# A hybrid decoder layer on one core: equal tile offsets modulo 1024 bytes, first loads on one queue, the first norm's residual a block ahead

## The chip, the core and the metric

The kernel runs on one core of one Trainium2 chip. The metric is device time in microseconds (us) of one execution, the median of several runs. The engines spoken of are TensorE (PE, with its weight loads shown apart as PEld), VectorE (DVE), ScalarE (ACT), GpSimd (POOL) and SyncE (SP), which issues most DMAs in order from one queue.

## The reference, cut to what matters

One layer over 512 tokens of width 1024 in fp32. A combined projection feeds three token mixers: forgetting attention ("FoX", 8 heads), a Mamba-2 scan ("SSD") and a complex diagonal state space model ("S5"). Each mixer's output is projected, gated and summed, and goes through an output projection. A norm with residual, a gated MLP (5632 up columns, width-3 convolution, 2816 down rows) and a second norm follow:

```python
proj = x @ w_in
q, k, v, f_logit, z, xbc, dt_raw, u, gate_logit = jnp.split(proj, _split_points(), axis=-1)
merged = jnp.sum(gates * jnp.einsum('blrw,rwd->blrd', branches, w_branch), axis=2)
x1  = layer_norm(ALPHA * x  + merged @ w_out, ln1_g, ln1_b)
ffn = (silu(gate) * val) @ w_down          # val, gate = split(causal_dwconv(x1 @ w_up))
out = layer_norm(ALPHA * x1 + ffn, ln2_g, ln2_b)
```

## The kernel before, in words

**Arithmetic.** Each fp32 operand of a big product is split into a high part (fp32r) and the rest, and a product takes three matmuls, hi·hi, hi·lo and lo·hi. `mm3` (lines 173 to 175) is that triple with the weight tile as the stationary operand (128 x 128) and a 512-column activation tile moving. `gemm_N` (lines 279 to 281) is the triple the other way round: a 128-column slice of x is stationary and a weight tile moves; so are the output projection (lines 1193 to 1195) and the down projection (lines 1250 to 1252).

**Where operands lie.** Four pools share each partition of SBUF, one after the other: the "ring" (`ringp`: 5 tiles `whi` and 5 tiles `wlo` of 4096 bytes, into which the stream of weights is split), `tiny` (small tiles, each taking 32 bytes or a multiple; one of them is `mn`), `xpool` (4 tiles of 8192 bytes: the split input `xth`/`xtl`, later `x1Th`/`x1Tl`, at the end the weights `resh`/`resl`) and `half` (61 "slots" of 2048 bytes: everything else of 512 columns, the split activations `ya`, `yb`, `yc`, `gy`, `mT`, `hT` and the split output weights `wkh`/`wkl` among them). In the built programs:

| pool, tile | start, before | modulo 1024 | start, after | modulo 1024 |
|---|---|---|---|---|
| ring, first `whi` / `wlo` | 28,544 / 49,024 | 896 | 28,544 / 49,024 | 896 |
| xpool, first tile | 71,424 | 768 | 71,552 | 896 |
| slots, first | 104,192 | 768 | 104,320 | 896 |

All tiles of a pool have the same remainder, since their sizes are multiples of 1024. Within a tile a stationary slice starts at a multiple of 512 bytes and a moving row at a multiple of 2048.

**Stages.** `Stream` (lines 51 to 108) loads weight tiles in a fixed order on the SP queue into two raw buffers (`wraw`), splits each on ACT (high part, line 100) and DVE (rest, line 101), and runs a few tiles ahead. `fill_first` multiplies the first four weight tiles (`w_u`) by x as the eight tiles of x arrive: a step of it is one 128-row tile of x, with 14 matmuls. The projections follow, with the mixers' tasks put between them by a list of due units (lines 1344 on); then the merges, the output projection (`out_block`, four blocks of 128 tokens, 48 matmuls each), beside which `norm1` of the block before runs, and the MLP. A scheduler orders the instructions of each engine by priority; `tc.high_priority()` moves what stands in it ahead.

**At the start** x tile 0 is loaded on the ACT queue (line 233), the first weight tile in three pieces on SP (line 83), and between the second and third piece `W.between` (`second_x`) adds x tile 1 and the small weight `fdw`. **At the first norm** `norm1(b)` issues the two loads of its residual `xr` itself (line 1156), waits some steps, adds, takes the statistics, scales (`xh`), and later has PE transpose `xh` (line 1170) and stores it (`drx`, line 1181).

Of the kernel before, what the change touches and what calls it, by code (L numbers as in the profile page):

```python
# [16 lines left out]
P = 128  # L17
# [44 lines left out]
class Stream:  # L62
# [8 lines left out]
    def prefetch(self, n):  # L71
        nc = self.nc
        while self.made < min(n, len(self.plan)):
            key, src = self.plan[self.made]
            w = self.raw.tile([P, 1024], F32, name="wraw", tag="wraw")
            if self.made:
                nc.sync.dma_start(out=w, in_=src)
            else:

                hi = self.ring.tile([P, 1024], F32R, name="whi", tag="whi")  # L80
                lo = self.ring.tile([P, 1024], F32R, name="wlo", tag="wlo")
                for h_ in (slice(0, 256), slice(256, 512), slice(512, 1024)):
                    nc.sync.dma_start(out=w[:, h_], in_=src[:, h_])
                    nc.scalar.activation(hi[:, h_], w[:, h_], AF.Copy)  # L84
                    nc.vector.tensor_tensor(out=lo[:, h_], in0=w[:, h_], in1=hi[:, h_].bitcast(F32), op=ALU.subtract)
                    if h_.stop == 512:
                        self.between()
                r = (hi, lo)
            if key in self.keep:
                r = []  # L90
                for hf in range(2):
                    hi, lo = (self.slots.tile([P, 512], F32R, name="wk" + c_, tag="s2") for c_ in "hl")
                    ws = w[:, hf * 512:(hf + 1) * 512]
                    nc.scalar.activation(hi, ws, AF.Copy)
                    nc.vector.tensor_tensor(out=lo, in0=ws, in1=hi.bitcast(F32), op=ALU.subtract)
                    r.append((hi, lo))
            elif self.made:
                hi = self.ring.tile([P, 1024], F32R, name="whi", tag="whi")
                lo = self.ring.tile([P, 1024], F32R, name="wlo", tag="wlo")
                nc.scalar.activation(hi, w, AF.Copy)  # L100
                nc.vector.tensor_tensor(out=lo, in0=w, in1=hi.bitcast(F32), op=ALU.subtract)  # L101
                r = (hi, lo)
            self.out.append(r)
            self.made += 1
# [9 lines left out]
def hybrid_trunk_kernel(ctx: ExitStack, tc: tile.TileContext, a, out):  # L114
# [18 lines left out]
    def s2(shape, dt=F32, name="s2"):  # L133
        return half.tile(list(shape), dt, name=name, tag="s2")
# [15 lines left out]
    def tt(o, x, y, op, eng=None):  # L150
        (eng or dve).tensor_tensor(out=o, in0=x, in1=y, op=op)  # L151
# [69 lines left out]
    def load_x(k):  # L221
        xraw[k] = s2([P, L], name="xraw")
        sp.dma_start(out=xraw[k], in_=a["xT"][k])
# [4 lines left out]
    wps = ps([P, P])  # L228
    for i in range(7):
        pe.matmul(wps, wz, wz, start=True, stop=True)  # L230
    with tc.high_priority():
        xraw[0] = s2([P, L], name="xraw")
        act.dma_start(out=xraw[0], in_=a["xT"][0])
        dve.tensor_copy(xp[0][0], xraw[0])  # L234
        tt(xp[0][1], xraw[0], xp[0][0].bitcast(F32), ALU.subtract)

    def second_x():
        with tc.high_priority():
            load_x(1)
            sp.dma_start(out=fdw, in_=a["w_fd"])  # L240
            split(fd[:, :, 0:16], fd[:, :, 16:32], fdw)
        split(xp[1][0], xp[1][1], xraw[1])

    W.between = second_x
    W.prefetch(1)
    load_x(2)
    split(xp[2][0], xp[2][1], xraw[2])
# [405 lines left out]
    def s5_run(qt):  # L653
        while qt not in s5m:
            yield 1
        u_load(qt)
        yield 4
        mm_, it, om, er, ei, rho = s5m.pop(qt)
        uu = s5u.pop(qt)
        v = ps([P, 8, 64])  # L660
        for g in range(8):
            pe.matmul(v[:, g, :], it[g], uu[:, g, :], start=True, stop=True)
        yield 1
        vs = s2([P, 8, 64], name="s5V")
        act.copy(vs[LOH], v[HIH])
        act.copy(vs[HIH], v[LOH])
        yield 2
        w = s2([P, 8, 64], name="s5W")
        tt(w, v, er, ALU.mult)
        tt(vs, vs, ei, ALU.mult)  # L670
        tt(w, w, vs, ALU.add)
        sc = s2([P, 512], name="s5S")
        dve.tensor_tensor_scan(out=sc, data0=rho.rearrange("p a c -> p (a c)"), data1=w.rearrange("p a c -> p (a c)"),
                               initial=0.0, op0=ALU.mult, op1=ALU.add)
        yield 3
        sw = s2([P, 512], name="s5Sw")
        act.copy(sw[LOH], sc[HIH])
        act.copy(sw[HIH], sc[LOH])
        xx = s2([P, 8, 64], name="s5X")
        dve.memset(xx[:, :, 0:1], 0.0)  # L680
        sv, swv = (m.rearrange("p (a c) -> p a c", c=64) for m in (sc, sw))
        x1_, c63 = xx[:, :, 1:64], slice(0, 63)
        tt(x1_, sv[:, :, c63], er[:, :, c63], ALU.mult)
        tt(swv[:, :, c63], swv[:, :, c63], ei[:, :, c63], ALU.mult)
        tt(x1_, x1_, swv[:, :, c63], ALU.subtract)
        yield 6
        y = ps([P, 8, 64])
        for g in range(8):
            pe.matmul(y[:, g, :], mm_[g], uu[:, g, :], start=True, stop=False)
            pe.matmul(y[:, g, :], om[g], xx[:, g, :], start=False, stop=True)  # L690
        ysb = s2([P, 8, 64], name="s5Y")
        act.copy(ysb, y)
        yield 4
        dry = tc.dram_tile([P, 512], F32, name="dry%d" % qt)
        dst = dry.rearrange("(g h) (t c) -> t h g c", h=16, c=64)
        for t in range(8):
            sp.dma_start(out=dst[7 - t], in_=ysb[16 * t:16 * t + 16])
        yield 3
        yt = s2([P, 512], name="s5yt")
        sp.dma_start(out=yt, in_=dry)  # L700
        yield 3

        g1, g2 = s2([P, 512]), s2([P, 512], name="s5g2")
        tt(g1, yt, yt, ALU.mult, pool)
        ts(g1, g1, 0.044715, ALU.mult, 1.0, ALU.add, eng=pool)
        tt(g1, g1, yt, ALU.mult, pool)
        yield 6
        act.activation(g1, g1, AF.Tanh, scale=GELU_C)
        gy = pair("gy")
        stt(g2, g1, 1.0, yt, ALU.add, ALU.mult)  # L710
        split(gy[0], gy[1], g2)
        s5y[qt] = (g2, gy)
        yield 1
# [241 lines left out]
    def fox_min(u):  # L955
        n = (fox_units[u][1] + 1) * P
        sc = fx.pop(("rel", u))
        mn = tmp([P, 1], "mn", 7)
        dve.tensor_tensor_reduce(out=sc, in0=fx.pop(("ps", u)), in1=sc, scale=1.0, scalar=3e38,
                                 op0=ALU.add, op1=ALU.min, accum_out=mn)  # L960
        fx["sc", u] = sc, mn
# [166 lines left out]
    def output_and_ffn():  # L1128
# [12 lines left out]
        def bn(bs, hf, r):  # L1141
            dve.bn_stats(out=bs[:, hf, :], in_=r)

        def norm_scalars(bs):
# [4 lines left out]
            tt(rs, rs, mhalf[:, 0:1], ALU.pow, pool)  # L1149
            return mv[:, 0:1], rs  # L1150

        def norm1(b, o):
            xr = [s2([P, 512], name="xr") for _ in range(2)]
            bs = tmp([P, 2, 6], "bs", 4)
            for hf in range(2):
                sp.dma_start(out=xr[hf], in_=a["x"][b * P:(b + 1) * P, HS[hf]])
            yield 3
            for hf in range(2):
                stt(xr[hf], xr[hf], ALPHA, o[hf], ALU.mult, ALU.add)
                bn(bs, hf, xr[hf])  # L1160
            mean, rs = norm_scalars(bs)
            xh = [s2([P, 512], name="xh") for _ in range(2)]
            for hf in range(2):
                ts(xh[hf], xr[hf], mean, ALU.subtract, rs, ALU.mult)
            yield 9
            t = slice(b * P, (b + 1) * P)
            for hf in range(2):
                tp = ps([P, 4, P])
                for kk in range(4):
                    pe.transpose(tp[:, kk, :], xh[hf][:, kk * P:(kk + 1) * P], ident)  # L1170
                f = s2([P, 4, P], name="x1f")
                for kk in range(4):
                    k = 4 * hf + kk
                    if kk % 2:
                        act.activation(f[:, kk, :], tp[:, kk, :], AF.Identity, scale=col("ln1_g", k),
                                       bias=col("ln1_b", k))
                    else:
                        ts(f[:, kk, :], tp[:, kk, :], col("ln1_g", k), ALU.mult, col("ln1_b", k), ALU.add)
                split(x1g[hf][0][:, :, t], x1g[hf][1][:, :, t], f)
            for hf in range(2):  # L1180
                sp.dma_start(out=drx[b][:, HS[hf]], in_=xh[hf])
            yield 1
# [16 lines left out]
        def advance(g):  # L1199

            if g is not None:
                if g[1] <= 1:
                    g[1] = next(g[0], 99)
                else:
                    g[1] -= 1

        wo, prev = [], None
        for b in range(NB):
            gen = out_block(b, wo)
# [281 lines left out]
```

## Time and profile before

| | us |
|---|---|
| median of 3 runs | 882.29 |
| lowest and highest | 881.64, 882.63 |
| the profiled execution, its own time | 881.78 |
| its span, first to last instruction | 880.0 |
| PE busy in the span | 866.8 |
| DVE, ACT, POOL busy | 590.9, 378.9, 63.1 |

The page gives each engine's busy time, the groups of like instructions, and a chain of waits traced back from the last instruction. Matmuls are pipelined: a row's duration reaches past the start of the next, so the cost of one in a stream is read from the distance between starts in the timeline, not from its duration. A row of the timeline has its start and duration in us, then engine, line, operation and tiles, and in brackets what ended an idle time before it.

### The profile page before, as it was taken

The page shows a single profiled execution, that of the slowest core. Times are in us where ns is not written, and L with a number is a line of the kernel's source. Part 1 is how long each engine was busy: PE and PEld are TensorE (multiplying, and loading weights), DVE is VectorE, ACT ScalarE, POOL GpSimd, SP SyncE. Part 2 cuts the span into 40 slices and gives each one's busy share as a digit, 9 for nine tenths or more (in the row PEclk, how much of TensorE's full clock was granted, in tenths as well). Part 3 has the DMA queues.
Part 4 walks back from the last instruction along what each step waited for, and adds up shares of the span by engine and source line. Part 5 has one row for each costly group of instructions (what it writes and reads, how often), then busy time and mean ns, then how long its engine had stood idle before and what let it go on. Part 6 is the DMA issues. An engine that isn't in the chain of part 4 may idle for free.

```text
span 880.0 us, 11393 instructions
## 1 busy us (share of the span) xinstructions
PE 866.8 (98%) x4211; PEld 716.5 (81%) x4211; DVE 590.9 (67%) x1022; ACT 378.9 (43%) x629; POOL 63.1 (7%) x144
## 2 busy tenths in 40 slices
PE   9999999999999999999999999999999999999996
PEld 7788788888888888788887898888888888888885
DVE  5898987885779866777667667557755555556217
ACT  5625235453656876763225244433333333343100
POOL 0370000000202220100000000000000000000001
PEclk9999999999999999999999999999999999999999
DMA  7615443424512543262516323253422222226102
GB/s 260 226 46 172 127 145 98 134 67 139 192 55 81 189 144 112 69 214 72 191 55 235 142 83 110 95 165 122 144 96 96 96 95 86 93 90 213 48 1 96
DMA packets 58648, 107.63 MB, mean 122 GB/s; under 512 B 21824, under 2 KB 27712, under 8 KB 58592
## 3 DMA queue, kind: packets, MB, share of 16 engines
q1 hardware_dynamic: 55568, 101.66, 34.6%
q10 hardware_dynamic: 3024, 5.24, 1.6%
q8 instruction: 33, 0.54, 0.3%
q14 instruction: 23, 0.19, 0.1%
HBM read 95.35 MB, written 11.53 MB: 121 GB/s over the span
## 4 chain that ended last, share of the span: by engine, by line
PE 92%; DVE 4%; issue 1%; DMA 1%; ACT 1%; POOL 0%; DVEq 0%; POOLq 0%
PE acc L173 20%; PE acc L174 20%; PE acc L175 20%; PE ps L1252 3%; PE ps L1250 3%; PE ps L1251 3%; PE acc L1250 2%; PE acc L1251 2%; PE acc L1252 2%; PE acc L279 2%; PE acc L281 2%; PE acc L280 2%; PE acc L1193 1%; PE acc L1194 1%; PE acc L1195 1%
## 5 line engine op out<-in xcount | busy, mean ns | idle before, releaser
L101 DVE TENSOR_TENSOR wlo<-wraw,whi 128x1024 fp32r<-128x1024 f32 x125 | 154.3, 1235 | 113.8 <-ACT whi L100 113.6
L100 ACT ACTIVATE whi<-wraw 128x1024 fp32r<-128x1024 f32 x125 | 132.1, 1058 | 183.8 <-PE acc L174 130.0
L173 PE MATMUL acc<-x1Th,whi 128*128 128x512 f32 (+1 forms) x384 | 144.4, 376 | 0.0
L174 PE MATMUL acc<-x1Tl,whi 128*128 128x512 f32 (+1 forms) x384 | 144.3, 376 | 0.0
L175 PE MATMUL acc<-x1Th,wlo 128*128 128x512 f32 (+1 forms) x384 | 144.2, 376 | 0.0
L173 PE MATMUL acc<-xth,whi 128*128 128x512 f32 x336 | 134.8, 401 | 0.6 <-DVE xth L234 0.6
L174 PE MATMUL acc<-xtl,whi 128*128 128x512 f32 x336 | 133.6, 398 | 0.0
L175 PE MATMUL acc<-xth,wlo 128*128 128x512 f32 x336 | 133.5, 397 | 0.0
L175 PEld LDWEIGHTS acc<-x1Th,wlo 128*128 128x128 f32 x384 | 72.3, 188 | 14.2
L174 PEld LDWEIGHTS acc<-x1Tl,whi 128*128 128x128 f32 x384 | 72.4, 188 | 14.1
L173 PEld LDWEIGHTS acc<-x1Th,whi 128*128 128x128 f32 x384 | 72.3, 188 | 14.0
L173 PEld LDWEIGHTS acc<-xth,whi 128*128 128x128 f32 x336 | 63.7, 190 | 15.7 <-ACT whi L84 0.9
L174 PEld LDWEIGHTS acc<-xtl,whi 128*128 128x128 f32 x336 | 63.7, 190 | 14.2 <-issue 0.4
L175 PEld LDWEIGHTS acc<-xth,wlo 128*128 128x128 f32 x336 | 63.5, 189 | 14.3
L160 DVE SCALAR_TENSOR_TENSOR cv<-acc,cols,cv 128x511 f32<-128x511 f32 (+1 forms) x88 | 65.4, 746 | 2.8 <-ACT cv L1229 1.5
L151 POOL TENSOR_TENSOR lrs<-lrs,mhalf 128x1 f32<-128x1 f32 x8 | 5.9, 731 | 476.7 <-DVE lrs L155 476.7
L1252 PE MATMUL ps<-whi,hTl 128*128 128x512 f32 (+1 forms) x102 | 38.7, 379 | 0.0
L1250 PE MATMUL ps<-whi,hTh 128*128 128x512 f32 (+1 forms) x102 | 38.6, 379 | 0.0
L1251 PE MATMUL ps<-wlo,hTh 128*128 128x512 f32 (+1 forms) x102 | 38.6, 379 | 0.0
L1229 ACT ACTIVATE cv<-acc,cols 128x512 f32<-128x512 f32 x44 | 33.5, 763 | 1.9 <-PE acc L175 1.9
L1237 ACT ACTIVATE cv<-cv 128x512 f32<-128x512 f32 x22 | 13.9, 632 | 41.6 <-DVE cv L160 41.6
L160 DVE SCALAR_TENSOR_TENSOR gate<-gate,acc 128x512 f32<-128x512 f32 x24 | 16.5, 686 | 16.8 <-PE acc L175 16.8
(318 smaller groups left out, 1553.2 us busy)
## 6 DMA issues: line engine op xcount, KB each, us to landing
wraw<-w_up SPq DMA_DIRECT2D x44, 512.0 KB, 3.2
wraw<-w_gate SPq DMA_DIRECT2D x24, 512.0 KB, 3.2
wraw<-w_dn SPq DMA_DIRECT2D x22, 512.0 KB, 3.2
wraw<-w_branch SPq DMA_DIRECT2D x12, 512.0 KB, 3.2
drt<-gate ACTq DMA_DIRECT2D x18, 256.0 KB, 2.3
gate<-drt SPq DMA_DIRECT2D x18, 256.0 KB, 5.1
wraw<-w_out SPq DMA_DIRECT2D x8, 512.0 KB, 3.2
wraw<-w_xbc SPq DMA_DIRECT2D x6, 512.0 KB, 4.2
```

The source lines that it names most:

```text
L100: nc.scalar.activation(hi, w, AF.Copy)
L101: nc.vector.tensor_tensor(out=lo, in0=w, in1=hi.bitcast(F32), op=ALU.subtract)
L160: dve.scalar_tensor_tensor(out=o, in0=x, scalar=s, in1=y, op0=op0, op1=op1)
L173: pe.matmul(o, w[0], x[0], start=first, stop=False)
L174: pe.matmul(o, w[0], x[1], start=False, stop=False)
L175: pe.matmul(o, w[1], x[0], start=False, stop=last)
L279: pe.matmul(o[b], xh, wh[:, s], start=(k == 0), stop=False)
L280: pe.matmul(o[b], xh, wl[:, s], start=False, stop=False)
L1229: act.activation(r, o, AF.Identity, scale=col("ffn_w", w0 + 2), bias=col("ffn_b", ch))
L1250: pe.matmul(o, hh, wh, start=(k == 0), stop=False)
L1251: pe.matmul(o, hh, wl, start=False, stop=False)
L1252: pe.matmul(o, hl, wh, start=False, stop=(k == NF - 1))
```

## The change

It has five parts. (1) `mn` gets 11 buffers in place of 7. The four more take 4 x 32 = 128 bytes of `tiny`, so that xpool and slots start 128 bytes further on; the ring stays (table above). (2) x tile 0 is loaded on SP after the first weight piece, x tile 1 after the third piece and the next whole weight tile. (3) In `norm1` the residual of block b+1 is loaded when block b's norm begins (block 0's before the output projection). (4) That norm's arithmetic up to `xh` is put under high priority, without the pause of three steps before it. (5) In `s5_run` a pause before the GELU is 4 units, not 3.

```diff
@@ Stream.prefetch
-                for h_ in (slice(0, 256), slice(256, 512), slice(512, 1024)):
+                for n_, h_ in enumerate((slice(0, 256), slice(256, 512), slice(512, 1024))):
...
-                    if h_.stop == 512:
-                        self.between()
+                    if n_ < 2:
+                        self.between(n_)
@@ hybrid_trunk_kernel
-    with tc.high_priority():
-        xraw[0] = s2([P, L], name="xraw")
-        act.dma_start(out=xraw[0], in_=a["xT"][0])
-        dve.tensor_copy(xp[0][0], xraw[0])
-        tt(xp[0][1], xraw[0], xp[0][0].bitcast(F32), ALU.subtract)
-
-    def second_x():
+    def early(n_):
         with tc.high_priority():
-            load_x(1)
-            sp.dma_start(out=fdw, in_=a["w_fd"])
-            split(fd[:, :, 0:16], fd[:, :, 16:32], fdw)
-        split(xp[1][0], xp[1][1], xraw[1])
-
-    W.between = second_x
+            if n_ == 0:
+                load_x(0)
+                dve.tensor_copy(xp[0][0], xraw[0])
+                tt(xp[0][1], xraw[0], xp[0][0].bitcast(F32), ALU.subtract)
+            else:
+                sp.dma_start(out=fdw, in_=a["w_fd"])
+                split(fd[:, :, 0:16], fd[:, :, 16:32], fdw)
+                load_x(1)
+        if n_:
+            split(xp[1][0], xp[1][1], xraw[1])
+
+    W.between = early
@@ s5_run
         sp.dma_start(out=yt, in_=dry)
-        yield 3
+        yield 4
@@ fox_min
-        mn = tmp([P, 1], "mn", 7)
+        mn = tmp([P, 1], "mn", 11)
@@ output_and_ffn
+        xrs = {}
+        def xr_load(b):
+            xrs[b] = [s2([P, 512], name="xr") for _ in range(2)]
+            for hf in range(2):
+                sp.dma_start(out=xrs[b][hf], in_=a["x"][b * P:(b + 1) * P, HS[hf]])
+
         def norm1(b, o):
-            xr = [s2([P, 512], name="xr") for _ in range(2)]
+            xr = xrs.pop(b)
+            if b + 1 < NB:
+                xr_load(b + 1)
             bs = tmp([P, 2, 6], "bs", 4)
-            for hf in range(2):
-                sp.dma_start(out=xr[hf], in_=a["x"][b * P:(b + 1) * P, HS[hf]])
-            yield 3
-            for hf in range(2):
-                stt(xr[hf], xr[hf], ALPHA, o[hf], ALU.mult, ALU.add)
-                bn(bs, hf, xr[hf])
-            mean, rs = norm_scalars(bs)
-            xh = [s2([P, 512], name="xh") for _ in range(2)]
-            for hf in range(2):
-                ts(xh[hf], xr[hf], mean, ALU.subtract, rs, ALU.mult)
+            with tc.high_priority():
+                for hf in range(2):
+                    stt(xr[hf], xr[hf], ALPHA, o[hf], ALU.mult, ALU.add)
+                    bn(bs, hf, xr[hf])
+                mean, rs = norm_scalars(bs)
+                xh = [s2([P, 512], name="xh") for _ in range(2)]
+                for hf in range(2):
+                    ts(xh[hf], xr[hf], mean, ALU.subtract, rs, ALU.mult)
             yield 9
...
+        xr_load(0)
         wo, prev = [], None
```

The built programs show what moves at the two places of which the prediction speaks. The first is the start. On SP, the queue of loads, the kernel before has this order (xraw_108 is x tile 1, wraw_122 the second weight tile, xraw_118 x tile 2):

```order
L83 DMA wraw_99<-w_u 128x256
L223 DMA xraw_108<-xT 128x512
L240 DMA fdw_83<-w_fd 128x128
L83 DMA wraw_99<-w_u 128x256
L83 DMA wraw_99<-w_u 128x512
L77 DMA wraw_122<-w_u 128x1024
L223 DMA xraw_118<-xT 128x512
```

After the change SP has at the start (xraw_101 is x tile 0, xraw_111 x tile 1):

```order
L83 DMA wraw_95<-w_u 128x256
L223 DMA xraw_101<-xT 128x512
L238 DMA fdw_83<-w_fd 128x128
L83 DMA wraw_95<-w_u 128x256
L83 DMA wraw_95<-w_u 128x512
L77 DMA wraw_122<-w_u 128x1024
L223 DMA xraw_111<-xT 128x512
```

x tile 0 has taken the place of x tile 1, and x tile 1 now stands behind the second weight tile. On PE, at the second step of `fill_first` (x tile 1; acc_146 to acc_149 are the four products), the changed program has this order, where before each product's triple stood together behind both lines 307 and 308:

```order
L307 MATMUL ps_145<-xth_79,fd_84 32x512
L173 MATMUL acc_146<-xth_79,whi_96 128x512
L173 MATMUL acc_147<-xth_79,whi_96 128x512
L173 MATMUL acc_148<-xth_79,whi_96 128x512
L173 MATMUL acc_149<-xth_79,whi_96 128x512
L308 MATMUL ps_145<-xtl_80,fd_84 16x512
L174 MATMUL acc_146<-xtl_80,whi_96 128x512
```

The five matmuls that need only the high part of x tile 1 come first, then those that need its rest. The second place is the output projection with the first norm. On SP the difference is (- before, + after; `xr` are residual loads, `drx` the stores of the normed blocks):

```order
-L77 DMA wraw<-w_out 128x1024 x8
+L77 DMA wraw<-w_out 128x1024 x5
+L1157 DMA xr<-x 128x512 x2
+L77 DMA wraw<-w_out 128x1024 x3
 L77 DMA wraw<-w_up 128x1024
-L1156 DMA xr<-x 128x512
+L1157 DMA xr<-x 128x512
 L77 DMA wraw<-w_up 128x1024
-L1156 DMA xr<-x 128x512
-L77 DMA wraw<-w_up 128x1024 x3
-L1181 DMA drx_4656<-xh 128x512 x2
-L1156 DMA xr<-x 128x512 x2
```

Block 0's residual now stands among the output weights, and block 1's, which stood behind block 0's store, stands among the first MLP weights. On DVE the norm of block 0 reads after the change (xr_4660 and xr_4661 are its residual halves, wlo_4749 a weight tile of the MLP):

```order
L160 SCALAR_TENSOR_TENSOR xr_4660<-xr_4660,acc_4664 128x512
L160 SCALAR_TENSOR_TENSOR xr_4661<-xr_4661,acc_4665 128x512
L1142 BN_STATS bs_4786<-xr_4660 128x6
L1142 BN_STATS bs_4786<-xr_4661 128x6
L101 TENSOR_TENSOR wlo_4749<-wraw_4746,whi_4748 128x1024
L1146 BN_AGGR mv_4791<-bs_4786 128x2
L155 TENSOR_SCALAR lrs_4793<-mv_4791 128x1
L157 TENSOR_SCALAR xh_4796<-xr_4660,mv_4791,lrs_4793 128x512
L157 TENSOR_SCALAR xh_4797<-xr_4661,mv_4791,lrs_4793 128x512
```

One weight split stands inside the norm, where before there were two and a third ahead of it. On PE block 0's last matmul is the 72nd of the output projection (before: the 68th) and its transposes follow the 96th (before: the 106th); block 1's follow the 144th (before: the 145th).

## Rows read from the trace of the kernel before

**Rows 1.** The page, busy us (share of the span) and instructions.
```profile
PE 866.8 (98%) x4211; PEld 716.5 (81%) x4211; DVE 590.9 (67%) x1022; ACT 378.9 (43%) x629; POOL 63.1 (7%) x144
```
**Rows 2.** Groups on PE by shape: count | busy us, mean ns | idle before.
```profile
L173 PE MATMUL acc<-xth,whi 128*128 128x512 f32 x336 | 134.8, 401 | 0.6 <-DVE xth L234 0.6
L173 PE MATMUL acc<-x1Th,whi 128*128 128x512 f32 x320 | 126.3, 395 | 0.0
L1250 PE MATMUL ps<-whi,hTh 128*128 128x512 f32 x88 | 34.7, 395 | 0.0
L279 PE MATMUL acc<-whi,xth 128*128 128x512 f32 x64 | 25.5, 401 | 0.7 <-DVE cv L160 0.7
L1250 PE MATMUL acc<-whi,hTh 128*128 128x512 f32 x42 | 16.6, 395 | 0.0
L173 PE MATMUL acc<-yah,whi 128*128 128x512 f32 x32 | 12.7, 398 | 0.1
L173 PE MATMUL acc<-gyh,whi 128*128 128x512 f32 x16 | 6.4, 399 | 0.0
```
**Rows 3.** Timeline of PE in the MLP, ring against xpool: start us, duration.
```profile
604.16 0.39 PE L173 MATMUL acc<-x1Th,whi 128*128 128x512 f32 x1
...
617.87 0.39 PE L175 MATMUL acc<-x1Th,wlo 128*128 128x512 f32 x1
```
**Rows 4.** Timeline of PE in the last down projection, xpool against slots.
```profile
851.81 0.39 PE L1250 MATMUL acc<-resh,hTh 128*128 128x512 f32 x1
...
865.41 0.39 PE L1250 MATMUL acc<-resh,hTh 128*128 128x512 f32 x1
```
**Rows 5.** Busy us (count) in two stretches: PE, PEld, DVE, ACT, POOL, clock, DMA.
```profile
491.00:501.00 10.00, 10.00 (x46) 8.28 (x45) 6.27 (x13) 2.87 (x6) 0.54 (x1) 1.00 0.40 138
600.00:700.00 100.00, 100.00 (x432) 81.09 (x431) 58.63 (x72) 36.30 (x47) 0.00 (x0) 1.00 0.33 111
```
**Rows 6.** Timeline of PE in the output projection, slots against slots, after transposes.
```profile
478.64 1.08 PE L1170 MATMUL ps<-ident,xh 128*128 128x128 f32 x8
...
479.80 0.40 PE L1195 MATMUL acc<-wkh,mTl 128*128 128x512 f32 x1
...
481.66 0.39 PE L1194 MATMUL acc<-wkl,mTh 128*128 128x512 f32 x1
...
483.93 0.39 PE L1195 MATMUL acc<-wkh,mTl 128*128 128x512 f32 x1
```
**Rows 7.** Timeline of the start, all engines (ACTq, SPq: DMA issues).
```profile
0.71 0.41 ACTq L233 DMA_DIRECT2D xraw<-xT  x1
...
1.15 0.43 SPq L223 DMA_DIRECT2D xraw<-xT  x1
...
4.46 0.43 DVE L234 CAST xth<-xraw 128x512 fp32r<-128x512 f32 x1 [3.47 <-DMA xraw<-xT]
...
5.04 0.76 PE L173 MATMUL acc<-xth,whi 128*128 128x512 f32 x1 [0.64 <-DVE xth L234]
...
6.02 0.61 ACT L165 ACTIVATE xth<-xraw 128x512 fp32r<-128x512 f32 x1
...
8.91 1.06 ACT L100 ACTIVATE whi<-wraw 128x1024 fp32r<-128x1024 f32 x1 [0.64 <-DMA wraw<-w_u]
...
10.00 1.23 DVE L101 TENSOR_TENSOR wlo<-wraw,whi 128x1024 fp32r<-128x1024 f32 x1 [1.00 <-ACT whi L100]
...
10.38 0.39 PE L307 MATMUL ps<-xth,fd 128*32 128x512 f32 x1
```
**Rows 8.** Timeline of the norm of block 1: SP, DVE, PE.
```profile
479.43 1.20 SPq L1156 DMA_DIRECT2D xr<-x  x2
...
484.76 0.69 DVE L160 SCALAR_TENSOR_TENSOR xr<-xr,acc 128x512 f32<-128x512 f32 x1 [1.04 <-DMA xr<-x]
...
489.07 1.00 DVE L157 TENSOR_SCALAR xh<-xr,mv,lrs 128x512 f32<-128x512 f32 x2 [0.67 <-POOL lrs L151]
...
489.77 1.09 PE L1170 MATMUL ps<-ident,xh 128*128 128x128 f32 x8 [1.14 <-DVE xh L157]
```

## The prediction

> **What bounds the kernel now.** I read the page first: PE is busy for 866.8 of 880.0 us [rows 1], so nearly all the time is the sum of the distances between matmuls, and 13 us at most are waits. I then listed PE's groups by shape, to see how many matmuls there are of each kind, walked PE's timeline for the distance from start to start, and looked at the few places where PE stood still. Durations would mislead here: a 128x512 matmul is shown with about 395 ns [rows 2], but the next starts long before its end.
>
> **Part 1, the offsets.** In the MLP the moving operand lies in xpool (remainder 768) and the stationary one in the ring (896). From the first to the last row there are 59 steps [rows 3]: (617.87 - 604.16) / 59 = 232.4 ns each. In the last down projection the moving operand lies in xpool and the stationary one in a slot (both 768); from the first to the last row there are 60 steps [rows 4]: (865.41 - 851.81) / 60 = 226.7 ns. That is 5.7 ns less for the same shape and type. It is not the work of the other engines: in 491 to 501 us, where both operands are slots, DVE is busy for 63% and ACT for 29%, and PE still starts 46 matmuls in or across 10 us; in 600 to 700 us, with ring operands, DVE is busy for 59%, ACT for 36%, and PE starts only 432 in 100 us [rows 5]. Nor does it hang on an exact match: in rows 4 the stationary slices start at 0, 512, 1024 and 1536 bytes of their tile, block after block, at one distance all along. After the change every ring, xpool and slot operand stands as in rows 4 (remainder 896 throughout).
>
> How many matmuls this touches: each line of rows 2 is one of a triple, so (336 + 320 + 88 + 64 + 42) x 3 = 2550, the merges are three kinds like the ya line, 3 x 32 x 3 = 288, and the GLU adds 16 x 3 = 48. That makes 2886 of 128x512; at 5.7 ns, 16.5 us at most.
>
> Not all of them will get it. After a break (transposes, a small matmul) the short distance comes back only after some steps: the 8 steps from 479.80 to 481.66 take 1.86 us, 232.5 ns each, and the 10 steps to 483.93 take 2.27 us, 227 ns each [rows 6]. Walking PE's timeline I count 88 breaks in the streams that the change touches, most of them between 10 and 412 us, where the mixers' small matmuls stand among the projections. 88 x 8 x 5.7 ns = 4.0 us are lost so. The term is **-12.5 us**, with -16.5 (no break costs anything) and 0 as its ends. A loss I leave out, since the matmuls that already run at equal offsets are the quicker ones. PE is the bound and nothing else fills the time: DVE's 590.9 us [rows 1] leave it a third of the span, so it can follow a PE that is 1.5% quicker.
>
> The Trainium skill speaks against this term. "TensorE: Matmul & The Clock Gate", section "Step-by-step: what each phase is for", says that PE reads its moving operand and its weights through two independent ports, and that loading the next weights takes no read bandwidth from the running matmul; its section "Back-to-back issue gap" gives a gap of N/2.4 + 2.5 ns, 216 ns for 512 columns, whatever the addresses. By it this term would be 0. The trace does not agree on either count: it shows two distances, 232.4 and 226.7 ns, and neither is 216. What the page leaves possible is that the two differ for another reason than the offset, and that is the first rival below.
>
> **Part 2, the start.** PE's first real matmul starts at 5.04 us, after the split of x tile 0 that began at 4.46, when the tile had landed; its load was issued on ACT at 0.71, beside the SP queue's, where x tile 1 was issued at 1.15 [rows 7]. After the change tile 0 has SP's second place and no load competes with it but the first weight piece ahead of it. It may land up to 0.8 us sooner (the competing 256 KB of tile 1 are gone) or, if a second place lands as tile 1 did, be split as late as 6.02 [rows 7], 1.5 us later. What decides is the second step, though. It began at 10.38 and its 14 matmuls take 14 x 0.232 = 3.25 us, to 13.63. After the change tile 1 comes behind the second weight tile in SP, ACT and DVE. That weight tile was split from 8.91 on; 256 KB fewer are ahead of it now, some 0.65 us, so from about 8.25. ACT then takes 1.06 + 0.61 us (weight, tile 1), to 9.92, and DVE 1.23 us from about 9.35 for the weight and 0.69 for tile 1's rest, to 11.27 [rows 7, 8] (the 0.69 is taken from an operation of the same shape in the norm). PE runs the five high-part matmuls in between, to 11.1, and the other nine to 11.27 + 9 x 0.232 = 13.36. That is **-0.3 us**. Bounds: -1.0 if everything lands early; above, the first step took 5.34 us for 14 matmuls (5.04 to 10.38), 2.1 more than later ones, and if the wait for tile 1 makes the second step as slow, the term is +1.8.
>
> On the move to one queue the skill's "DMA: Bandwidth & Descriptors", section "Issuing engines are not separate DMA queues", says that a second issuing engine saves only the time of the issue. By it tile 0 would come later by 1.15 - 0.71 = 0.44 us, and the first matmul with it. No row of before shows the two orders side by side; the second step's sum holds either way, as it rests on tile 1.
>
> **Parts 3 and 4, the norm.** At 489.77 PE had waited 1.14 us for block 1's `xh` [rows 8]. The cause is upstream: the residual was issued at 479.43, behind block 0's store, and DVE could not add before 484.76 [rows 8]. Block 1's matmuls had ended long before: PE ran 49 more (49 x 0.227 = 11.1 us) and block 0's transposes (1.08 [rows 6]) between them and 488.63, so they ended at about 476.4. With the residual there the chain of add, statistics and scale (484.76 to 489.07 + 1.00, less a foreign 0.69: 4.6 us) can end by 481 or 482, 5 us before PE wants it. So this wait goes, -1.1. What is late next is block 0's: its last matmul is now the 72nd and its transposes follow the 96th, so 24 x 0.227 = 5.4 us cover a chain of 4.6 plus the weight split of 1.23 inside it, 5.8: +0.4. The loads on SP cost nothing as long as block 0's residual is issued while SP waits for raw buffers anyway (the sixth output weight waits for DVE's splits). Block 3's chain has 54 half-width matmuls (some 0.12 each, half of 0.23) and block 2's transposes as cover, 6.5 + 1.1 us. The term is **-0.7 us**, between -1.4 (block 0 costs nothing and a second, shorter wait goes too) and +0.5 (block 1's chain is late again by half of it).
>
> **Part 5.** The GELU's inputs are needed by the GLU much later, and POOL has 63 us of work in 880 [rows 1]: 0, with about 1 us either way for the order of the mixers' instructions on DVE and ACT that this shifts, since PE waits on those chains at times.
>
> **Sum.** -12.5 - 0.3 - 0.7 = -13.5 us. The profiled execution took 881.78 in all (its span is 880.0, and 1.8 lie around it), so 868.3; it stands 0.5 below the median of before (882.29), so **868.8 us** on the scale of the medians, 1.5% faster.
>
> **Rivals.** (a) *It is the ring, not the offset.* Every slow pair has one operand in the ring, and no fast pair has; the ring is also lower in memory and written whole tile by whole tile. If that is the reason, part 1 gives nothing, and parts 2 to 4 leave 882.3 - 1.0 = 881.3 us. For it: rows 3 and 4 can't separate the two. Against it: ring tiles and slots are parts of one memory, read by the same instructions, and the engines that write them were as busy in the quick stretch of rows 5 as in the slow one. 13%. This is also the skill's case above. (b) *Half of it.* The short distance may hold only where both slices match modulo 1024; a stationary slice of the ring moves on by 512 bytes with every triple, unlike rows 4, where it stays for 24 matmuls. The lock would then be lost and found at each step, for about half the gain: 868.8 + 6.3 = 875.1. 7%. (c) *The start is lost.* x tile 1 stands behind 512 KB that PE doesn't need yet. If it comes so late that the second step starts late and runs as slowly as the first, that costs 1.8; if tile 0 is also split at 6.02, 1.5 more. With part 1 at nothing and the norm's -0.9, the time is 882.3 + 3.3 - 0.7 = 884.9 us, slower; it decides only where (a) holds too, from a start that loses 0.7 + 1.8 = 2.5 us. For it: the order on SP. Against it: the weight tile ahead was split at 8.91, before PE wanted tile 1. 4%.
>
> **How the numbers follow.** My forecast has 76%; its own range is 864.5 to 871.5 (part 1 between -16.5 and -10, the start, the norm and the mixers' order by their bounds). The range with (b) reaches 876, and 18% or so is left outside. Within 0.2% (1.8 us) is what a measurement of this kernel can't tell from no change: (a) falls there for the most part, so faster 86%, same 9%, slower 5%.
>
> **What would show it right or wrong.** In the MLP the distance from start to start should be 227 ns over a long stretch, also in `gemm_N` and the merges; 232 there is (a), a mix is (b). The first matmul should start by 4.5 us and the second step end by 13.4; a gap of over 1 us before line 308 is (c). The transposes of block 1 should follow their matmul without a wait, and block 0's wait by under 1 us. Above 876 us part 1 is wrong; below 864 the breaks cost nothing, or PE gained where I saw no wait.

## The result and the profile after

The changed kernel takes 866.97 us (median of 4 runs, 866.3 to 867.87) against 882.04 us before (four runs; the table ahead has 882.29 from three): ratio 0.9829, 95% interval 0.9812 to 0.9846. 868.8 us was forecast. The profiled execution took 867.87 us, the longest of the four, with a span of 866.1 us. Three marks on PE's timeline cut both traces, and those of the experiments that change one part, into stretches (the first matmul of line 342, which ends the fill; the first of the output projection; the last one):

| us | to line 342 | to the output projection | from there to the last matmul |
|---|---|---|---|
| before | 38.82 | 414.83 | 418.07 |
| after | 40.82 | 408.17 | 408.71 |
| after, another execution | 38.72 | 408.27 | 408.64 |
| before with 11 `mn` buffers | 38.37 | 407.58 | 411.33 |
| after with 7 `mn` buffers | 39.20 | 414.54 | 416.49 |
| after with the norm of before | 38.93 | 408.43 | 411.74 |
| after with the start of before | 38.75 | 408.17 | 408.74 |
| after with x tile 1 behind x tile 0 | 37.31 | 407.13 | 408.66 |

So after gains 6.7 and 9.4 us in the second and third stretch and loses 2.0 in the first; another execution of it loses nothing there (38.72). The page still has PE at 98%, 15.2 us less busy than in [rows 1] with as many instructions:

```profile
PE 851.6 (98%) x4211; PEld 715.6 (83%) x4211; DVE 586.2 (68%) x1022; ACT 379.0 (44%) x629; POOL 64.1 (7%) x144
```

PE's timeline in the MLP of after, ring against xpool (start us, duration), two rows 59 steps apart, answers to [rows 3]:

```profile
649.95 0.39 PE L173 MATMUL acc<-x1Th,whi 128*128 128x512 f32 x1
...
663.32 0.39 PE L175 MATMUL acc<-x1Th,wlo 128*128 128x512 f32 x1
```

(663.32 - 649.95) / 59 = 226.6 ns, where before had 232.4: the distance of [rows 4], now with a ring operand. The last down projection, whose operands stood equally before, keeps its distance of [rows 4], (851.39 - 837.79) / 60 = 226.7 ns:

```profile
837.79 0.39 PE L1258 MATMUL acc<-resh,hTh 128*128 128x512 f32 x1
...
851.39 0.39 PE L1258 MATMUL acc<-resh,hTh 128*128 128x512 f32 x1
```

Behind a break the long step remains. In the output projection of after, as in [rows 6], the 8 steps from 472.10 take 1.85 us, 231 ns each, and the next 10 take 2.27, 227 each. The transposes ahead of them follow their matmul without a named wait:

```profile
471.00 1.04 PE L1177 MATMUL ps<-ident,xh 128*128 128x128 f32 x8
...
472.10 0.39 PE L1201 MATMUL acc<-wkl,mTh 128*128 128x512 f32 x1
...
473.95 0.39 PE L1200 MATMUL acc<-wkh,mTh 128*128 128x512 f32 x1
...
476.22 0.39 PE L1201 MATMUL acc<-wkl,mTh 128*128 128x512 f32 x1
```

The start, which answers to [rows 7], is where after loses. Its timeline, all engines:

```profile
4.20 0.43 DVE L235 CAST xth<-xraw 128x512 fp32r<-128x512 f32 x1 [3.20 <-DMA xraw<-xT]
...
4.77 0.69 PE L173 MATMUL acc<-xth,whi 128*128 128x512 f32 x1 [0.38 <-ACT fd L165]
...
8.38 0.39 PE L175 MATMUL acc<-xth,wlo 128*128 128x512 f32 x1
...
9.53 1.06 ACT L100 ACTIVATE whi<-wraw 128x1024 fp32r<-128x1024 f32 x1 [0.66 <-DMA wraw<-w_u]
...
10.49 2.92 ACT L165 ACTIVATE xth<-xraw 128x512 fp32r<-128x512 f32 x5
...
11.16 0.42 PE L307 MATMUL ps<-xth,fd 128*32 128x512 f32 x1 [2.38 <-ACT xth L165]
...
12.98 0.63 PE L174 MATMUL acc<-xtl,whi 128*128 128x512 f32 x1
```

PE starts 0.27 us sooner and ends its first step at 8.6 instead of 10.4, but then stands for 2.4 us: x tile 1 is split at 10.49, behind the second weight tile, and not at 6.02. Behind the wait the matmuls start 0.43 us apart in place of 0.23 (the one behind the last row starts at 13.41). The windows of after show the granted clock there (columns as in [rows 5]; the clock is the number ahead of the last two):

```profile
12.00:14.00 2.00, 2.00 (x7) 1.29 (x6) 2.00 (x4) 1.40 (x3) 0.00 (x0) 0.52 0.97 305
14.00:16.00 2.00, 2.00 (x8) 1.49 (x7) 1.18 (x3) 1.41 (x2) 0.00 (x0) 0.63 0.96 365
```

At 0.52 the clock is near the lower of its two levels, 1.2 GHz. The other execution of the same kernel waited 1.8 us in this place, and the clock stayed up:

```profile
10.44 0.42 PE L307 MATMUL ps<-xth,fd 128*32 128x512 f32 x1 [1.77 <-ACT xth L165]
...
12.00:14.00 2.00, 2.00 (x10) 1.52 (x9) 2.00 (x4) 0.77 (x2) 0.00 (x0) 1.00 0.86 226
```

That one ended the fill at 38.72 us, against 40.82. The norm of after, [rows 8] in before: first on SP block 0's residual (448.86) and the two halves of block 1's, each issued 7 us or more before DVE reads it (465.30 and 472.02), then DVE's chain for block 0:

```profile
448.86 0.86 SPq L1157 DMA_DIRECT2D xr<-x  x2
...
461.79 0.43 SPq L1157 DMA_DIRECT2D xr<-x  x1
...
464.99 0.33 SPq L1157 DMA_DIRECT2D xr<-x  x1
...
465.30 1.37 DVE L160 SCALAR_TENSOR_TENSOR xr<-xr,acc 128x512 f32<-128x512 f32 x2 [1.08 <-PE acc L1202]
...
469.96 1.00 DVE L157 TENSOR_SCALAR xh<-xr,mv,lrs 128x512 f32<-128x512 f32 x2 [0.67 <-POOL lrs L151]
```

DVE now waits for PE's products and not for the residual. The list of PE's waits of after is empty from 445 to 515 us, where before has one, for `xh`.

### The profile page after: what moved, and what is told of

It reads as the page before. It is cut to its first block, busy times and chain, and to the rows that moved or that the text cites. A ratio compares the mean times of both kernels' runs of the same rounds, so it can differ in the third digit from the quotient of the medians.

```text
span 866.1 us, 11400 instructions
## 1 busy us (share of the span) xinstructions
PE 851.6 (98%) x4211; PEld 715.6 (83%) x4211; DVE 586.2 (68%) x1022; ACT 379.0 (44%) x629; POOL 64.1 (7%) x144
## 4 chain that ended last, share of the span: by engine, by line
PE 95%; DVE 2%; ACT 1%; DMA 1%; issue 1%; SPq 0%; DVEq 0%
PE acc L174 20%; PE acc L175 20%; PE acc L173 20%; PE ps L1260 3%; PE ps L1259 3%; PE ps L1258 3%; PE acc L1259 2%; PE acc L1258 2%; PE acc L1260 2%; PE acc L279 2%; PE acc L1201 2%; PE acc L1202 2%; PE acc L1200 2%; PE acc L280 2%; PE acc L281 2%; PE ps L1013 1%
## 5 line engine op out<-in xcount | busy, mean ns | idle before, releaser
L173 PE MATMUL acc<-xth,whi 128*128 128x512 f32 x336 | 132.9, 397 | 0.4 <-ACT fd L165 0.4
L174 PEld LDWEIGHTS acc<-x1Tl,whi 128*128 128x128 f32 x384 | 72.3, 188 | 12.5
L1245 ACT ACTIVATE cv<-cv 128x512 f32<-128x512 f32 x22 | 13.9, 633 | 41.6 <-DVE cv L160 41.6
L959 DVE CUSTOM_DVE_ANT_0 rel<-ps,rel 128x128 f32<-128x128 f32 (+3 forms) x32 | 15.6, 487 | 18.7 <-PE ps L952 12.8
```

The source lines that it names most:

```text
L173: pe.matmul(o, w[0], x[0], start=first, stop=False)
L174: pe.matmul(o, w[0], x[1], start=False, stop=False)
```

## The experiments

**Is it the offset?** Five kernels put one distance each between ring and x tiles. The kernel before with the one line of the offset:

```
-        mn = tmp([P, 1], "mn", 7)
+        mn = tmp([P, 1], "mn", 11)
```

> The kernel before with eleven mn buffers in place of seven and nothing else, so ring, x tiles and slots stand at equal remainders; start, norm and yield as before. Theory A (equal offsets shorten the step from start to start): MLP steps of 226.7 ns, 2284 steps that are 8 or more behind a break gain 5.7 ns and 548 nearer ones some 2 ns, in all -14.1 us: 882.0 - 14.1 = 867.9 us. Rival B (the start, the norm or the ring's place do it): 882 us, steps of 232.4 ns. Rival C (four more mn buffers take waits away, not the offset): also 868, but with steps of 232.4 ns and fewer waits between 252 and 412 us.

Measured: 867.36 us, ratio 0.9839 (0.9824 to 0.9853), with steps of 226.8 ns:

```profile
649.53 0.39 PE L173 MATMUL acc<-x1Th,whi 128*128 128x512 f32 x1
...
662.91 0.39 PE L175 MATMUL acc<-x1Th,wlo 128*128 128x512 f32 x1
```

The one line alone gives about as much as the whole change; the rival that it is the ring falls, since the operands are still in the ring. The wait for `xh` is still there in its list of PE's waits (us in total, times, longest), 445 to 515 us:

```profile
PE ps L1170 <- DVE xh L157: 1.2, 1, 1.2
PE acc L1193 <- ACT wkh L94: 0.3, 1, 0.3
```

The other way round, after with the line undone (11 to 7):

> The kernel after with seven mn buffers, so that x tiles and slots stand 128 bytes short of the ring's remainder again; all else as after. Theory A: 867.0 + 14.1 = 881.1 us, MLP steps of 232.4 ns; the start 2.3 us later than before, the norm 1.9 us quicker. Rival B: 867 us. Rival C: 881, with the difference in waits between 252 and 412 us and not in the MLP.

Measured: 880.71 us, ratio 0.9993 (0.9983 to 1.0002): without the offset the rest of the change can't be told from nothing. Its start loses only 0.4 us against before (39.20 against 38.82), not the 2.3 expected: PE waited 1.7 us there, and the granted clock stayed at 1.00. The steps are 233.2 ns:

```profile
603.91 0.39 PE L173 MATMUL acc<-x1Th,whi 128*128 128x512 f32 x1
...
617.67 0.40 PE L175 MATMUL acc<-x1Th,wlo 128*128 128x512 f32 x1
```

The next three keep eleven buffers and move tiny tiles from behind the ring to ahead of it. The edit is the same in all, with other names in the list:

```
+    tiny0 = ctx.enter_context(tc.tile_pool(name="tiny0", bufs=1))
     ringp = ctx.enter_context(tc.tile_pool(name="ringp", bufs=5))
...
-        return tiny.tile(list(shape), F32, name=name, tag=name, bufs=bufs)
+        return (tiny0 if name in ('rc', 'ea', 'de', 'cd') else tiny).tile(list(shape), F32, name=name, tag=name, bufs=bufs)
```

With `rc` alone the ring is 64 bytes off:

> The kernel after (eleven mn buffers kept); two tiny tiles of 64 bytes in all stand in front of the ring, so that the ring's remainder is 64 bytes off that of x tiles and slots. Theory A (remainders must be equal): 867.0 + 14.1 = 881.1 us, MLP steps of 232.4 ns. Rival C (the buffers, not the offset) and rival D (only a distance of 128 bytes or more hurts): 867 us, steps of 226.7 ns.

Measured: 879.4 us, ratio 0.9976 (0.9966 to 0.9985); steps of (618.17 - 604.40) / 59 = 233.4 ns:

```profile
604.40 0.39 PE L174 MATMUL acc<-x1Th,whi 128*128 128x512 f32 x1
...
618.17 0.39 PE L176 MATMUL acc<-x1Th,wlo 128*128 128x512 f32 x1
```

So it is not the number of buffers, and 64 bytes are enough to lose it. With the four names above, 256 bytes:

> The kernel after (eleven mn buffers kept); eight tiny tiles of 256 bytes in all stand in front of the ring, so that the ring's remainder modulo 1024 is 256 bytes off that of x tiles and slots. Theory A in the form that the remainder modulo 512 or more must match: 881.1 us, MLP steps of 232.4 ns. Rival E (only the remainder modulo 256 or less must match): 867 us, steps of 226.7 ns. Rival C: 867 us.

Measured: 866.86 us, ratio 0.9837 (0.9818 to 0.9855), steps of 226.6 ns, though the remainders modulo 1024 are 128 and 896:

```profile
604.04 0.39 PE L174 MATMUL acc<-x1Th,whi 128*128 128x512 f32 x1
...
617.41 0.39 PE L176 MATMUL acc<-x1Th,wlo 128*128 128x512 f32 x1
```

Equal offsets modulo 1024 are thus more than is needed. Whether 256 bytes either way suffice, or a multiple of them is wanted, a last kernel tells, with `ss` and `rs` in the list too, 384 bytes:

> The kernel after (eleven mn buffers kept); twelve tiny tiles of 384 bytes in all stand in front of the ring, so that the ring's remainder is 384 bytes off, that is 128 modulo 256. Theory (the remainders modulo 256 must match): 866.9 + 14 = 881 us, MLP steps of 232.4 ns. Rival (a distance of 256 bytes or more either way is enough): 867 us, steps of 226.7 ns.

Measured: 880.56 us, ratio 0.9995 (0.9981 to 1.001), steps of 233.2 ns:

```profile
604.15 0.39 PE L174 MATMUL acc<-x1Th,whi 128*128 128x512 f32 x1
...
617.91 0.40 PE L176 MATMUL acc<-x1Th,wlo 128*128 128x512 f32 x1
```

Distances of 64, 128 and 384 bytes are slow, 0 and 256 quick: of the five distances run, the quick ones are those at which the remainders modulo 256 match. In one place 64 bytes cost only about half: `gemm_N`, where the ring's tile moves, has 229.6 ns on the mean of its steps 8 or more behind a break (before 233.0, after 226.7). Why is open.

**The start.** After with the start of before:

```
-    def early(n_):
+    with tc.high_priority():
+        xraw[0] = s2([P, L], name="xraw")
+        act.dma_start(out=xraw[0], in_=a["xT"][0])
...
+    def second_x():
+        with tc.high_priority():
+            load_x(1)
```

> The kernel after with the start of the kernel before (x tile 0 on ACT's queue, x tile 1 second on SP's); offsets, norm and yield as after. Theory (the new start costs time, since x tile 1 is split at 10.49 us and not at 6.02): no wait ahead of the second step, its last matmul by 13.4 us; against the profiled run of after, whose clock also fell to 1.2 GHz behind the wait, 867.87 - 2.35 = 865.5 us, against those without that fall 866.4 - 0.7 = 865.7: 865.6 us, with all runs at one clock of 0.998. Rival (what the start loses is made up before 40 us, or the loss is of the profiled run alone): 867.0 us.

Measured: 866.07 us (864.54 to 868.71), ratio 0.9829 (0.9807 to 0.9851). The trace has the fill 2.1 us shorter than the profiled execution of after, near what was expected, but as long as the other one (38.75 against 38.72). The times spread by 4 us and the ratio is that of after: the two starts can't be told apart. x tile 1 moved up, still on one queue:

```
             else:
+                load_x(1)
                 sp.dma_start(out=fdw, in_=a["w_fd"])
                 split(fd[:, :, 0:16], fd[:, :, 16:32], fdw)
-                load_x(1)
```

> The kernel after, with x tile 1 issued right behind x tile 0 on SP, ahead of fdw and of the second and third piece of the first weight tile, and split in that place on ACT and DVE; still one queue. Theory (it is the place of x tile 1 that costs, not the single queue): no wait of over 1 us ahead of the second step; the second weight piece comes 256 KB, some 0.65 us, later, within the first step: 865.6 to 866.2 us. Rival (the single queue costs it): 867 us or more, the first step stretched to 10 us and beyond.

Measured: 864.2 us, ratio 0.9805 (0.9787 to 0.9824), below what was expected. Timeline of its start:

```profile
1.15 0.90 SPq L223 DMA_DIRECT2D xraw<-xT  x2
...
4.84 0.63 ACT L165 ACTIVATE xth<-xraw 128x512 fp32r<-128x512 f32 x1 [1.19 <-DMA xraw<-xT]
...
8.85 0.40 PE L307 MATMUL ps<-xth,fd 128*32 128x512 f32 x1
...
12.07 0.40 PE L307 MATMUL ps<-xth,fd 128*32 128x512 f32 x1
```

Tile 1 is split at 4.84, the second step runs from 8.85 to 12.07 without a wait, and the fill ends at 37.31. It was run again beside after:

> The kernel after with x tile 1 right behind x tile 0 on SP once more. If its start is worth what the trace showed (3.5 us at the end of the fill against an execution whose clock fell, some 1.5 against one whose clock did not), it is 1.5 to 3 us faster than after in this call; if chips and executions made the difference, equal to after within 0.5 us.

> The kernel after once more, beside the runs below on one chip. Ratio to before 0.983 as in its first runs; times in two groups some 1.3 us apart, with the granted clock 0.001 to 0.002 lower in the longer one, if the clock's fall behind the wait at the start comes in some executions only.

Measured: 864.55 us, ratio 0.981 (0.9795 to 0.9825), and after 866.83 us (865.67 to 869.09), ratio 0.9845 (0.9827 to 0.9863). They were measured side by side, 2.3 us apart with the intervals just apart: this version beats both kernels. Its fill ended at 37.24 this time. After's times did not fall into two clean groups (865.67 at a mean clock of 0.997; 866.67 to 869.09 at 0.995 and 0.996). To tell the wait from the clock, ten idle matmuls were put into the wait:

```
+                if k == 1:
+                    dps = ps([P, P])
+                    for _ in range(10):
+                        pe.matmul(dps, wz, wz, start=True, stop=True)
                 if k < KT - 1:
```

> The kernel after with ten more matmuls of the zero tile (128x128, into a bank of their own) on PE between the first and the second step of the fill, where after waits 2.4 us; nothing else. Theory (of the 2.35 us lost at the start, some 1.6 are the clock's fall to 1.2 GHz behind the wait, which comes in some executions only): the wait filled, the second step at 0.23 us a matmul in every run, all times within 0.3 us of one another at 866.3 to 866.5 us, clock 0.998. Rival (the clock falls for another reason, or the spread is the DMA's): times as after, 866.3 to 867.9, in two groups.

Measured: 867.6 us (866.96 to 867.86), ratio 0.9842 (0.9826 to 0.9859): the mean clock was 0.997 to 0.998 in all four runs, but no time was won. The trace shows two new waits:

```profile
8.69 2.39 PE L309 MATMUL ps<-wz 128*128 128x128 f32 x20
...
10.84 0.48 PE L311 MATMUL ps<-xth,fd 128*32 128x512 f32 x1
11.84 0.40 PE L312 MATMUL ps<-xtl,fd 128*16 128x512 f32 x1 [0.52 <-DVE xtl L151]
...
34.00 2.90 ACT L643 COPY up<-acc 128x512 f32<-128x512 f32 x3
35.07 0.19 PEld L173 LDWEIGHTS acc<-xth,whi 128*128 128x128 f32 x1 [1.22 <-ACT up L643]
```

The added matmuls made the second step take the low part of tile 1 second, where after has five others first; and at 35.07 PE waits for ACT to empty a bank. The fill ended at 41 us again (40.75). So with the wait filled the clock stayed up here, but as it also stayed up in one of after's two traces, one trace more does not prove the cause; nor does this run show what the fall alone costs.

**The norm and the yield.** After with the first norm of before (the residual loaded in the block's own turn, `yield 3` behind it, no priority):

> The kernel after with the first norm of the kernel before (residual loaded within the block's own turn, no priority for its chain). Theory (the earlier residual removed the wait for block 1's xh and others of the output projection, 1.9 us in the two traces): 867.0 + 1.9 = 868.9 us, with a wait of some 1.1 us ahead of block 1's transposes. Rival (most of the 1.9 is the arrival of the output weights, which the offsets or the fox stage set): 867.0 + 1.1 or less: 867.5 to 868.1 us.

Measured: 869.11 us, ratio 0.9868 (0.985 to 0.9886), as the theory had it. PE's waits from 445 to 515 us:

```profile
PE ps L1170 <- DVE xh L157: 1.5, 1, 1.5
PE acc L1193 <- ACT wkh L94: 0.2, 1, 0.2
```

The same chain is waited for here as in [rows 8] (1.14 us) and in the kernel before with 11 buffers (1.2). Last, after with `yield 3` in place of 4 in `s5_run`:

> The kernel after with the wait of the GELU's inputs at three turns in place of four, as before. Theory (that part is worth nothing beyond the order it shifts): within 1 us of after in this call. Rival (it is the later turn that makes the extra wait of 0.96 us at 300 us, ahead of the value product of the attention stage, which before does not have): 0.7 to 1 us faster than after, without that wait.

Measured: 865.62 us, ratio 0.9822 (0.9803 to 0.984), 1.2 us below after beside it, with overlapping intervals: unclear. The waits are clear. In after, 80 to 412 us, two of PE's four are for `mn`:

```profile
PE ps L1013 <- DVE mn L959: 0.7, 1, 0.7
...
PE ps L985 <- DVE mn L959: 0.3, 1, 0.3
```

The first of these is the one that the rival names, at 301 us ahead of the value product (line 1013). With `yield 3` both are gone, as the rival had it, and two stand there that before has too (there 0.7 and 0.5):

```profile
PE acc L279 <- DVE cv L160: 1.3, 1, 1.3
...
PE ps L836 <- DVE mn L959: 0.6, 1, 0.6
```

## Why the prediction was right

**Part 1, the offsets: right, a little too small.** -12.5 us were forecast. Counted step by step over the two traces, the 2284 steps that stand 8 or more behind a break went from 232.4 to 226.8 ns on the mean and 550 nearer ones from 232.5 to 230.4: 12.9 + 1.2 = 14.1 us. The mis-sized term is the breaks: they cost the whole difference for 8 steps in the sum (4.0 us), but the mean step shortens already from the third one on, and they cost 2.1. `gemm_N` and the merges, which the prediction also named, have 226.7 and 226.9 ns behind the breaks, from 233.0 and 232.4. The two kernels that move only this line show it from either side (14.7 us off 882.03; 13.7 between after's 866.97 and 880.71). The Trainium skill's case against the term, "TensorE: Matmul & The Clock Gate", sections "Step-by-step: what each phase is for" and "Back-to-back issue gap", where the formula for the gap has the columns alone in it, does not hold here: for 512 columns the same program gives 227 or 233 ns by where a tile stands. The 216 ns are that section's figure for an isolated matmul; for a stream at 512 columns it gives some 131 ns, which no trace here shows either. Whether the reads of the two operands get in each other's way, against the first of the two sections, is not shown.

**Rival (a)**, the ring, fell with the first experiment. **Rival (b)** asked for both slices to match modulo 1024, at half the gain; the gain is whole, and a distance of 256 is as quick as 0. That the ring's stationary slices move on by 512 bytes does no harm fits this.

**Part 2, the start: wrong.** -0.3 us were forecast, +1.8 at most; the profiled execution shows +2.0 at the end of the fill, and +2.4 with the 0.45 us that the offset gives there (38.37 in the kernel before with 11 buffers). The other execution, whose clock stayed up, shows +0.35 by the same count. The first matmul started at 4.77, not by 4.5, and the second step ended at 15.98 (13.88 in the other), not by 13.4. The step that failed is "That weight tile was split from 8.91 on; 256 KB fewer are ahead of it now, some 0.65 us, so from about 8.25". It was split at 9.53, and x tile 1 behind it at 10.49. In the nine traces that have this order the split starts at 8.81 to 9.53, in the three with the start of before at 8.25 to 9.11: with 256 KB fewer ahead it came no sooner. The 0.65 us were 256 KB at some 400 GB/s; the first 5 us moved much less, and after less than before:

```profile
0.00:5.00 5.00, 3.36 (x14) 3.06 (x14) 0.68 (x4) 1.70 (x2) 0.75 (x6) 1.00 0.54 178
```

```profile
0.00:5.00 5.00, 3.59 (x15) 3.32 (x15) 0.95 (x4) 2.01 (x3) 0.75 (x6) 1.00 0.39 130
```

After moved 48 GB/s less for 5 us, 0.24 MB, about the 256 KB that the order had taken from the front. All nine traces with this order have 114 to 142 GB/s there, all five others 172 to 179, those with tile 1 moved up on the same queue among them; why is open. Nor was a fall of the clock behind the wait in the sum. It makes most of the difference between the executions: with the shorter wait the second step took 3.4 us and not 4.8, and the fill ended at 38.72. Not the single queue costs this but the place of tile 1, as the version with tile 1 moved up shows: its fill ends at 37.31 and 37.24, against 38.37 and 38.75 with the start of before and 38.72 or more with that of after. (By the times it is quicker than after; against the start of before they overlap.) On the move to one queue, "DMA: Bandwidth & Descriptors", section "Issuing engines are not separate DMA queues", had let the first matmul come 0.44 us later; the trace does not agree with this estimate from the Trainium skill's rule: it came 0.27 us sooner, tile 0 being on the way for 3.0 us instead of 3.7. The loads beside it changed too, so the rule itself is not tested; with tile 1 right behind on the same queue the first matmul came at 4.63.

**Parts 3 and 4, the norm: right in kind, too small.** -0.7 us were forecast, down to -1.4. The stretch from the output projection on lost 9.4 us, of which 7.35 are the offsets' in the MLP (1350 of the steps above): -2.0. With the norm of before put back it is 3.0 us longer; against the kernel before with 11 buffers the change's other parts give 2.6 there, and without the offset 1.6. Block 1's wait went as forecast. Block 0's chain, for which I added 0.4, cost nothing: from 465.30 to 470.96 it took 5.7 us, as worked out, and the transposes started at 471.00, right behind the matmul at 470.76. What I had not counted is a place further ahead in before, where PE's steps stretch from 0.23 to 0.34 and more while it takes the last output weights (timeline of before):

```profile
464.08 0.40 PE L1195 MATMUL acc<-wkh,mTl 128*128 128x512 f32 x1
464.47 0.51 PE L1193 MATMUL acc<-wkh,mTh 128*128 128x512 f32 x1
464.81 0.88 PE L1194 MATMUL acc<-wkl,mTh 128*128 128x512 f32 x2
```

Some 0.6 us are lost there; after has two such steps, 0.28 and 0.34. The weights do not come sooner in after. The seventh of the eight is finished by these rows of DVE, first of before, then of after:

```profile
464.45 1.29 DVE L95 TENSOR_TENSOR wkl<-wraw,wkh 128x512 fp32r<-128x512 f32 x2 [0.85 <-ACT wkh L94]
...
460.10 1.29 DVE L95 TENSOR_TENSOR wkl<-wraw,wkh 128x512 fp32r<-128x512 f32 x2 [1.11 <-ACT wkh L94]
```

Counted from the first matmul of the output projection (453.65 and 448.99) that is 10.8 us in before and 11.1 in after. What changed is PE's order: it parts from that of before at the 39th matmul, just where the first step of 0.34 stands in before, and block 0's last matmul is the 72nd and not the 68th. All three traces with the norm of before, with the offset or without, have five or more steps of 0.33 us and longer here, and those with the new norm two at most. So the stretched steps go with the norm's part, not with the offset.

**Part 5: 0, as far as it can be told.** By the two traces it takes away two waits (1.3 and 0.6 us; the first is not in the kernel before with 11 buffers, which has `yield 3` too) and brings two others (0.7 and 0.3). Between the fill and the output projection the two traces with `yield 3` and equal offsets have 407.58 and 409.16 us, those with `yield 4` 407.13 to 409.77: no difference can be read from these.

The sum of the trace is 2.4 - 14.1 - 2.0 = -13.7, and -0.2 are left for the rest: 881.78 - 867.87 = 13.9. That the forecast of -13.5 came so near is in part luck: a start too good by 2.7 us stood against an offset and a norm too poor by 2.9. The main mechanism, the offset, is not luck. The median lies 0.9 lower; the other execution, at 865.67, shows a start that loses less. "Above 876 us part 1 is wrong" and the mark for (a), 232 ns in the MLP, were the right things to look at; the mark for (c), a gap of over 1 us, came true one line earlier than it was set (2.4 us ahead of line 307, 0.4 ahead of 308), without its price deciding anything. In (c)'s sum the norm is named with -0.9 and reckoned with -0.7.

## What to carry to other kernels

Where PE is the bound, take the distance between matmuls of one shape from the timeline, pool by pool, and not their durations; two distances for one shape are a reason to look at where the operands' tiles stand (here: at their starts modulo 256). A few bytes of padding moved 1.6% here, which the other edits together did not. In a start that waits for loads, what PE needs next goes ahead of what it needs later (2.3 us here, on one and the same queue), and the price of a wait there may include the clock behind it.

## What was not expected of the hardware

- The step of a 128x512 fp32r matmul is 226.6 to 226.8 ns in the MLP where the starts of the ring's tile and of the x tile are 0 or 256 bytes apart (modulo 1024), and 232.4 to 233.4 where they are 64, 128 or 384 apart. Other distances were not run, and which of PE's two reads gives way is not shown.
- Behind a wait of 2.4 us at the start the granted clock was 0.52 for the next stretch; behind one of 1.8 us, in another execution of the same program, 1.00. Over the eight traces with this order and nothing put into the wait, the clock fell behind the four longest waits (1.9 to 2.4 us) and stayed at 1.00 behind the other four (1.8, 1.7, 0.5 and none). So few traces show no limit. Matmuls 0.43 us apart stand also in the first step of all three traces with the start of before, where the row of the clock gives 1.00; what slows these is open.
